# Experts as one hand-synchronised section with a branch over the third tile of tokens

## The chip, the cores and the metric

The program runs on one core of a Trainium2 chip. The metric is device time in microseconds, lower is better. Five engines take part, each with its own queue of instructions: TensorE (PE: matmul, PEld: loading of the stationary operand), VectorE (DVE), ScalarE (ACT), GpSimd (POOL) and SyncE (SP), which issues nearly all transfers from HBM. Matmuls write to eight PSUM banks; the granted clock of PE is 1.00 where it runs at 2.4 GHz.

## The reference

A two-layer transformer block stands in front (`first_block`), then a second one of two layers, whose last part is a mixture of experts. All of it is float32; only this last part is touched by the change:

```python
def moe_swiglu(h, router, w_gate, w_up, w_down):
    B, T, D = h.shape                                   # 1, 256, 1024
    ht = h.reshape(B * T, D)
    probs = jax.nn.softmax((ht @ router).astype(F32), axis=-1)      # 8 experts
    top_p, top_i = lax.top_k(probs, TOP_K)                          # TOP_K = 2
    top_p = top_p / jnp.sum(top_p, axis=-1, keepdims=True)
    gates = jnp.sum(jax.nn.one_hot(top_i, N_EXPERTS, dtype=F32) * top_p[..., None], axis=1).astype(h.dtype)
    out = jnp.zeros_like(ht)
    for e in range(N_EXPERTS):
        out = out + gates[:, e:e + 1] * swiglu(ht, w_gate[e], w_up[e], w_down[e])   # 1024 -> 1536 -> 1024
    return out.reshape(B, T, D)
```

Each of the 256 tokens goes to two of eight experts, so 512 places are shared out; how many an expert gets depends on the inputs.

## The kernel before

Everything up to the experts (attention, convolution, dense feed-forward) is left as it is. In `moe` the router counts the tokens of each expert; `places` writes one-hot matrices `oh` (which token stands in which place of an expert), and `gather` picks the tokens of three experts at a time by matmul into `xg`. An expert has room for `CAP` = 96 tokens, three tiles of 32 (`C32`, `NT`). If some expert got more than 96, the whole of `experts` is done again for the places behind (line 1736, a branch of all engines on `mosti`, the largest count).

`up(e)` walks over eight k-steps of two weight tiles (gate and up, 128 x 1536). A tile of tokens is only 32 wide, so the four column groups of PE each take a quarter of the weight's columns: per weight tile 3 tiles x 4 groups = 12 products, of 384 columns each (256 for expert 0, a third of whose columns are computed ahead of the router by `first_up`). `turn(e)` transposes the result, `down(e)` multiplies by twelve weight tiles of 128 x 1024: eight products each, four of 512 columns for the first two tiles of tokens and four of 256 columns for the third. `scatter(e)` brings the result back to token order by matmul, and VectorE adds it, times the gate, to `x`. All products of `up` and `down` go through `product`, so the profile shows them on line 1587. Every tile of tokens is computed, filled or not.

The order on PE is that of the code (`manual_schedule`): up(0), turn(0), then for each e: up(e) with scatter(e-2) between its steps, down(e-1) with turn(e) in it. Loads are issued by SP in an order that the framework's scheduler sets, as are the waits. Up weights have eight buffers (`mw`, 768 KB each, 512 KB for expert 0), down weights sixteen of 512 KB (`raw`, `wh`, `wl`, which the stages before used as well).

Of the kernel before, what the change touches and what calls it, by code (L numbers as in the profile page):

```python
# [6 lines left out]
F32 = mybir.dt.float32  # L7
# [34 lines left out]
MW_BUFS = 8  # L42
# [179 lines left out]


# [5 lines left out]
def build(tc, a, out, stages=None):  # L229
# [7 lines left out]
    with ExitStack() as es:  # L237
# [1215 lines left out]
        def moe(more, head, next_head):  # L1453
            hT = nrm["h"]
            with tc.tile_pool(name="moe", bufs=1) as sp:
# [12 lines left out]
                mosti = sp.tile([P, 1], I32, name="mosti")  # L1468
                trib = sp.tile([P, 2, P], BF16, name="trib")
# [5 lines left out]
                def router():  # L1475
# [36 lines left out]
                    V.tensor_copy(mosti, most)  # L1512
                    yield
# [39 lines left out]
                banks = {}  # L1553

                def bank(kind):

                    b, at = banks[kind]
                    banks[kind] = (b, (at + 1) % len(b))
                    return b[at]

                def experts(base, mid):

                    oh = sp.tile([P, 2, NE, P], F32R, tag="oh", name="oh")

                    def places(e):
                        for t in range(2):
                            V.tensor_scalar(oh[:, t, e], slots[:, base : base + P], pos[:, t, e : e + 1],
                                            sel[:, t, e : e + 1], op0=OP.is_equal, op1=OP.mult)

                    first = (0, 3, NE - 3)  # L1570
                    for e in range(3):
                        places(e)
                    made, turned, back = {}, {}, {}

                    def gather(e):

                        for k0 in range(0, KT, 2):
                            for k in (k0, k0 + 1):
                                p = bank("up")[:, : 3 * CAP]
                                for n, (t, part) in enumerate((t, part) for t in range(2) for part in (xh, xl)):  # L1580
                                    T.matmul(p, part[:, t, k * P : (k + 1) * P], oh[:, t, e : e + 3, :CAP], start=n == 0, stop=n == 3)  # L1581
                                o, g = xg[k // 4][:, k % 4], nrm["g"][:, k : k + 1]
                                A.activation(o, grp(p, 3), AF.Copy, scale=g) if k % 2 else V.tensor_scalar_mul(o, grp(p, 3), g)
                            yield

                    def product(o, l, w, first, last):
                        T.matmul(o, l, w, start=first, stop=last, skip_group_check=True)  # L1587

                    def up(e):


                        lo = 512 if e in mid else 0
                        n = (DE - lo) // 4
                        o = [[bank("up") for _ in range(2)] for _ in range(NT)]
                        for k in range(KT):
                            for m in range(2):
                                w = sp.tile([P, DE], F32, tag="mw", name="mw", bufs=MW_BUFS)
                                nc.sync.dma_start(w[:, : 4 * n], a["mo_u"][(e * KT + k) * 2 + m][:, lo:])
                                for t in range(NT):
                                    for g in range(4):  # L1600
                                        product(o[t][m][g * C32 : (g + 1) * C32, :n], xg[k // 4][:, k % 4, e - first[e // 3], t * C32 : (t + 1) * C32],
                                                w[:, g * n : (g + 1) * n], k == 0, k == KT - 1)
                            yield
                        made[e] = []
                        for t in range(NT):
                            u = sp.tile([P, 384], F32, tag="u", name="u", bufs=3)
                            A.activation(u[:, :n], o[t][0][:, :n], AF.Silu)  # L1607
                            V.tensor_mul(u[:, :n], u[:, :n], o[t][1][:, :n])
                            made[e].append(u)

                    def turn(e):

                        uT = sp.tile([P, DE // P, CAP], F32, tag="uT", name="uT", bufs=2)
                        turned[e] = uT
                        k1 = 0
                        if e in mid:
                            k1 = 4
                            u = mid[e]
                            for k0 in (0, 2):
                                p = bank("up")  # L1620
                                for k in (k0, k0 + 1):
                                    n = 0
                                    for t in range(2):
                                        for part in u:
                                            T.matmul(p[:, (k - k0) * S : (k - k0 + 1) * S], part[:, t, k * P : (k + 1) * P],
                                                     oh[:, t, :2], start=k == k0 and n == 0, stop=n == 3,
                                                     skip_group_check=True)
                                            n += 1
                                A.copy(uT[:, k0 : k0 + 2], grp(p, 2)[:, :, :CAP])
                        c = (DE // P - k1) // 4  # L1630
                        for t, u in enumerate(made.pop(e)):
                            p = bank("up")
                            for i in range(c):
                                T.transpose(p[:, i * P : (i + 1) * P], u[:, i * P : (i + 1) * P], ident)
                            A.copy(uT[:, k1:, t * C32 : (t + 1) * C32].rearrange("p (g c) n -> p c g n", c=c),
                                   p[:, : c * P].rearrange("p (c g n) -> p c g n", c=c, g=4))
                        p = bank("up")
                        for t in range(2):
                            T.transpose(p[:CAP, t * P : (t + 1) * P], oh[:, t, e, :CAP].bitcast(F32), ident)
                        ohT = sp.tile([P, 2, P], F32R, tag="ohT", name="ohT", bufs=2)  # L1640
                        A.copy(ohT[:CAP], p[:CAP, :S].rearrange("p (t n) -> p t n", t=2))
                        back[e] = ohT

                    def down(e):


                        uT = turned.pop(e)
                        acc = [bank("dn"), bank("dn")]
                        nk = DE // P
                        H = 2 * Q  # L1650
                        w = []
                        for kk in range(nk):
                            if kk % 4 == 0:
                                raw = wbuf("raw", 2 * D, F32, RAW_BUFS)
# [13 lines left out]
                            if kk % 2:  # L1668
                                yield
# [107 lines left out]
```

## Time and profile before

| | us |
|---|---|
| median of 3 runs | 1665.96 (1664.64 to 1666.89) |
| the profiled execution: time | 1666.39 |
| the profiled execution: span, first to last instruction | 1664.5 |
| first product of expert 0 | 1244.85 |
| last products of expert 7 end, copies begin | 1649.45 |

The mean granted clock is 0.984. A row of the chain reads: start, duration, engine, the tile's name, line, number of instructions; each f32 product counts twice on PE, with a weight load for each, as the hardware makes two passes of it. `pj` and `sm` are the two kinds of PSUM banks. A `q` behind an engine's name is its sequencer, which works ahead of the engine itself.

### The profile page before, as it was taken

How to read it: one execution, taken by the hardware profiler on the slowest of the kernel's cores; microseconds unless marked ns; L12 is line 12 of the kernel's file. 1: busy time of each engine (PE TensorE's matmuls, PEld its weight loads, DVE VectorE, ACT ScalarE, POOL GpSimd, SP SyncE). 2: the span in 40 equal slices, each digit the busy share in tenths (PEclk: the TensorE clock that was granted, in tenths of full speed). 3: DMA queues.
4: the chain of work that ended last, by engine and by line, in shares of the span. 5: the costliest groups of instructions: out<-in, count | busy, mean ns of one | idle time of the engine just before them, and what ended most of it. 6: DMA issues, size and time to landing. Idle time of an engine off the chain costs nothing.

```text
span 1664.5 us, 29813 instructions
## 1 busy us (share of the span) xinstructions
PE 1589.7 (96%) x12500; PEld 1245.9 (75%) x12500; DVE 888.3 (53%) x1547; ACT 734.7 (44%) x1318; POOL 121.6 (7%) x150
## 2 busy tenths in 40 slices
PE   7999999999999999987989999987999999999997
PEld 6878999878789999986879998977875444444443
DVE  6667877766558776876565555776460111111112
ACT  6646655555656555655464444555450110101001
POOL 2110000021000000151100000151100000000000
PEclk9999999999999999998999999998999999999998
DMA  7433655555426554432145554432369989998962
GB/s 284 152 120 126 214 178 192 171 179 183 145 78 215 192 179 161 163 136 74 45 176 190 197 178 165 154 132 60 149 237 409 395 329 370 373 372 339 374 232 78
DMA packets 68798, 336.86 MB, mean 202 GB/s; under 512 B 12816, under 2 KB 16112, under 8 KB 48048
## 3 DMA queue, kind: packets, MB, share of 16 engines
q1 hardware_dynamic: 57648, 327.70, 54.4%
q10 hardware_dynamic: 10272, 3.25, 0.8%
q0 software_dynamic: 736, 3.93, 0.6%
q8 instruction: 100, 1.64, 0.4%
q14 instruction: 42, 0.34, 0.1%
HBM read 332.03 MB, written 2.82 MB: 201 GB/s over the span
## 4 chain that ended last, share of the span: by engine, by line
PE 83%; issue 6%; DVE 4%; ACT 4%; POOL 2%; DMA 1%; ACTq 0%; POOLq 0%; DVEq 0%
PE pj L323 13%; PE pj L321 13%; PE pj L322 13%; PE sm L1587 12%; PE pj L1587 10%; PE sm L323 4%; PE sm L322 4%; PE sm L321 4%; PE sm L432 2%; DVE wl L314 1%; ACT wh L313 1%; PE sm L1220 1%; PE pj L1581 1%; PE sm L1229 1%; ACT hTh L333 1%
## 5 line engine op out<-in xcount | busy, mean ns | idle before, releaser
L314 DVE TENSOR_TENSOR wl<-raw,wh 128x1024 fp32r<-128x1024 f32 (+1 forms) x352 | 420.2, 1200 | 173.6 <-ACT wh L313 171.3
L313 ACT CAST wh<-raw 128x1024 fp32r<-128x1024 f32 (+1 forms) x352 | 359.5, 1028 | 216.2 <-PE pj L322 101.6
L321 PE MATMUL pj<-hTh,wh 128*128 128x256 f32 x1192 | 336.2, 282 | 0.0
L322 PE MATMUL pj<-hTl,wh 128*128 128x256 f32 x1192 | 335.8, 282 | 0.0
L323 PE MATMUL pj<-hTh,wl 128*128 128x256 f32 x1192 | 335.1, 282 | 0.0
L321 PEld LDWEIGHTS pj<-hTh,wh 128*128 128x128 f32 x1192 | 227.1, 191 | 1.1
L322 PEld LDWEIGHTS pj<-hTl,wh 128*128 128x128 f32 x1192 | 227.2, 191 | 0.9
L323 PEld LDWEIGHTS pj<-hTh,wl 128*128 128x128 f32 x1192 | 226.7, 191 | 0.2
L1587 PE MATMUL pj<-mw,xg 128*32 128x384 f32 (+1 forms) x2048 | 183.5, 473 | 0.0
L321 PE MATMUL pj<-wh,hTh 128*128 128x512 f32 (+1 forms) x368 | 141.9, 387 | 3.1 <-DVE mixl L335 1.5
L323 PE MATMUL pj<-wh,hTl 128*128 128x512 f32 (+1 forms) x368 | 139.0, 380 | 3.1 <-DVE hTl L335 3.0
L322 PE MATMUL pj<-wl,hTh 128*128 128x512 f32 (+1 forms) x368 | 139.5, 381 | 0.0
L1587 PEld LDWEIGHTS pj<-mw,xg 128*32 128x32 f32 x2048 | 65.3, 110 | 90.3 <-issue 83.3
L322 PE MATMUL sm<-wl,ph 128*128 128x512 f32 x264 | 103.2, 391 | 0.0
L321 PE MATMUL sm<-wh,ph 128*128 128x512 f32 x264 | 103.1, 391 | 0.0
L1587 PE MATMUL sm<-mw,xg 128*32 128x384 f32 (+1 forms) x1024 | 102.7, 473 | 0.0
L323 PE MATMUL sm<-wh,pl 128*128 128x512 f32 x264 | 102.0, 391 | 0.0
L843 DVE SCALAR_TENSOR_TENSOR u<-pj,tab_f,u 128x254 f32<-128x254 f32 (+1 forms) x176 | 82.7, 478 | 19.9 <-ACT u L841 18.2
L1607 ACT ACTIVATE u<-pj 128x384 f32<-128x384 f32 (+1 forms) x16 | 7.6, 477 | 180.4 <-PE pj L1587 180.4
L321 PEld LDWEIGHTS pj<-wh,hTh 128*128 128x128 f32 x368 | 70.7, 192 | 15.4 <-ACT hTh L333 2.5
L323 PEld LDWEIGHTS pj<-wh,hTl 128*128 128x128 f32 x368 | 70.3, 191 | 15.5 <-DVE hTl L335 6.0
L322 PEld LDWEIGHTS pj<-wl,hTh 128*128 128x128 f32 x368 | 70.6, 192 | 9.3
(435 smaller groups left out, 2266.9 us busy)
## 6 DMA issues: line engine op xcount, KB each, us to landing
mw<-in_mo_u SPq DMA_DIRECT2D x112, 768.0 KB, 7.0
raw<-in_up SPq DMA_DIRECT2D x44, 1024.0 KB, 4.9
raw<-in_mo_d SPq DMA_DIRECT2D x24, 1024.0 KB, 6.9
raw<-in_dn SPq DMA_DIRECT2D x22, 1024.0 KB, 4.8
raw<-in_fg_u SPq DMA_DIRECT2D x22, 1024.0 KB, 4.8
raw<-in_od_b SPq DMA_DIRECT2D x18, 1024.0 KB, 4.8
raw<-in_hy_b SPq DMA_DIRECT2D x16, 768.0 KB, 4.3
raw<-in_hy_a SPq DMA_DIRECT2D x12, 1024.0 KB, 4.8
```

Of the source, the lines that this page charges most:

```text
L313: A.copy(h, r)
L314: V.tensor_sub(m, r, h.bitcast(F32))
L321: T.matmul(o, lh, rh, start=first, stop=False)
L322: T.matmul(o, lh, rl, start=False, stop=False)
L323: T.matmul(o, ll, rh, start=False, stop=last)
L333: A.activation(oh, src, AF.Copy, scale=g)
L432: T.matmul(q, hT[j][:, k, ts_], w[f][k][v], start=t + k + i == 0, stop=k == KT - 1 and i == 2, skip_group_check=True)
L843: V.scalar_tensor_tensor(u[:, g, sh:], q[:, : S - sh], cw[:, f, g, wi : wi + 1], u[:, g, sh:], op0=OP.mult, op1=OP.add)
L1220: T.matmul(pq[:, i * P : (i + 1) * P], Am[:, i], U[:, i], start=i == 0, stop=True, skip_group_check=True)
L1229: T.matmul(pu[:, i * P : (i + 1) * P], Tt[:, i], Q[:, i], start=i == 0, stop=True, skip_group_check=True)
L1581: T.matmul(p, part[:, t, k * P : (k + 1) * P], oh[:, t, e : e + 3, :CAP], start=n == 0, stop=n == 3)
L1587: T.matmul(o, l, w, start=first, stop=last, skip_group_check=True)
```

## The change

The eight experts become one section of code in which the kernel sets all waits itself. A class `Hand` records every operation with its engine, what it reads and what it writes; from that it derives semaphore counts and emits the instructions engine by engine, with one semaphore per engine and one per load buffer. An operation is now a whole group of instructions (on PE all products of a k-step, or of two down tiles), and waits and signals once. The section stands in `tile_critical`: it begins when all engines have come to it. `places` and the first `gather` stay outside.

The router's counts go to `manyi`, and PE reads the eight into registers ahead of the section. In `up` for k > 0, and in `down` for all but the first two weight tiles, the products of the third tile of tokens stand behind a branch of PE alone: they are done if the expert has more than 64 tokens. With fewer, that tile's PSUM keeps what the first step wrote (the tokens there are zeros). They stand ahead of the other tiles' products of the step. The order among operations is kept; loads have an order of their own (`more`), nine up buffers instead of eight, and all down tiles are loaded one by one. The rare repetition for counts over 96 uses the same code without the hand-set waits and without branches.

```diff
-MW_BUFS = 8
+UP_SLOTS = 9
+DN_SLOTS = 16
+class Hand:
+    def emit(self, nc, engines, last):
...
+        for name, e in engines:
+            seen = {}
+            for eng, waits, go, lane, n in self.ops:
+                if eng == name:
+                    for w, v in waits.items():
+                        if v > seen.get(w, 0):
+                            e.wait_ge(sems[w], v)
+                            seen[w] = v
+                    go().then_inc(sems[lane], n)
+            if name == "SP":
+                for lane in last:
+                    e.wait_ge(sems[lane], self.count[lane])
...
+                    V.tensor_copy(manyi, p[:, 2 * NE : 3 * NE])
...
+                        self.order, self.busy = [("u", 0, j) for j in range(UP_SLOTS)], set()
+                    def more(self):
+                        d, u = [("d", 0, j) for j in range(nk)], [("u", 0, j) for j in range(UP_SLOTS, 2 * KT)]
+                        self.order, d = self.order + d[:4], d[4:]
+                        while u or d:
+                            self.order += u[:1] + d[:1]
+                            u, d = u[1:], d[1:]
+                        for e in range(1, NE):
+                            self.order += [("u", e, j) for j in range(2 * KT)]
+                            if e > 1:
+                                self.order += [("d", e - 1, j) for j in range(nk)]
+                        self.order += [("d", NE - 1, j) for j in range(nk)]
+                        self.feed()
...
+                    def third(self, e, go):
+                        if self.many is None:
+                            return go()
+                        with T.If(self.many[e] > 2 * C32):
+                            go()
...
+                            def go(k=k, tiles=tiles):
+                                if k == 0:
+                                    return tiles(range(NT))
+                                self.third(e, lambda: tiles((2,)))
+                                return tiles((0, 1))
+                            self.op("PE", go, [*w, ("xg", k)], [b for bs in o for b in bs])
+                            self.used(w)
...
+                            def go(k0=k0, halves=halves, quarters=quarters):
+                                self.third(e, quarters) if k0 else quarters()
+                                return halves()
...
-                        for g in range(4):
-                            o, p = y[2 * C32 : CAP, g * Q : (g + 1) * Q], acc[1][g * C32 : (g + 1) * C32, :Q]
-                            V.tensor_copy(o, p) if g % 2 else A.copy(o, p)
+                                (("ACT", "DVE")[g % 2], y[2 * C32 : CAP, g * Q : (g + 1) * Q], banks[b1][g * C32 : (g + 1) * C32, :Q], b1)
+                                for g in range(4)]:
...
+                main = Experts(0, mid, at_once)
+                with tc.manual_schedule(engines=MAN):
+                    main.places()
+                    main.feed()
+                    rest(main.gather(0))
+                main.many = [nc.values_load(manyi[:1, e : e + 1], engines=[mybir.EngineType.PE], min_val=0, max_val=S) for e in range(NE)]
+                hand = Hand()
+                main.op = hand.op
+                main.more()
+                main.run()
+                with tc.tile_critical():
+                    hand.emit(nc, (("SP", nc.sync), ("ACT", A), ("DVE", V), ("PE", T)), [("out", t, n) for t in range(2) for n in range(2)])
```

On PE, the end of up(1) and the beginning of down(0) read so before; L1587 is `product`, `mw` the up weights, `raw` and `wh` the down weights, and the shape 32x384 is that of one product:

```order
L1587 MATMUL pj<-mw,xg 32x384 x8
L1587 MATMUL sm<-mw,xg 32x384 x4
L1587 MATMUL pj<-mw,xg 32x384 x4
L1587 MATMUL sm<-raw,uT 32x512 x4
L1587 MATMUL sm<-raw,uT 32x256 x4
```

The same place now; L1712 are the up products, L1802 and L1795 the down products of the third tile and of the other two, L1671 the branch:

```order
L1671 COMPARE_AND_BRANCH
L1712 MATMUL pj<-up_12149,xg 32x384 x4
L1712 MATMUL pj<-up_12150,xg 32x384 x4
L1671 UNCONDITIONAL_BRANCH
L1712 MATMUL pj<-up_12149,xg 32x384 x4
L1712 MATMUL sm<-up_12149,xg 32x384 x4
L1712 MATMUL pj<-up_12150,xg 32x384 x4
L1712 MATMUL sm<-up_12150,xg 32x384 x4
L1802 MATMUL sm<-wh,uT_12141 32x256 x4
L1802 MATMUL sm<-wl,uT_12141 32x256 x4
```

The third tile's products of both weight tiles of a step have moved to its front, between a condition and a jump.

On SP, the loads of expert 0 and those behind them read so before (line 1598 loads up weights, lines 1655 and 1659 down weights; the first eight up tiles and sixteen down tiles stand ahead of this):

```order
L1659 DMA wl<-in_mo_d 128x1024
L1659 DMA wh<-in_mo_d 128x1024
L1598 DMA mw<-in_mo_u 128x1024 x8
L1598 DMA mw<-in_mo_u 128x1536 x24
L1655 DMA raw<-in_mo_d 128x2x1024
```

Now, with the section's beginning (line 1942 is the jump into it, for which SP waits for all engines; all loads are on line 1662):

```order
L1894 NO_OP
L1942 UNCONDITIONAL_BRANCH
L1662 DMA wh<-in_mo_d 128x1024
L1662 DMA wl<-in_mo_d 128x1024
L1662 DMA wh<-in_mo_d 128x1024
L1662 DMA wl<-in_mo_d 128x1024
L1662 DMA up_12146<-in_mo_u 128x1024
L1662 DMA wh<-in_mo_d 128x1024
L1662 DMA up_12147<-in_mo_u 128x1024
L1662 DMA wl<-in_mo_d 128x1024
```

The down tiles, which were sent before the experts began, have moved behind the section's beginning, among the remaining seven up tiles of expert 0.

On PE, between the last products of the gather and the first of expert 0, there is now this (line 1889 reads a count into a register; five more such reads stand among the gather's products):

```order
L1689 MATMUL pj<-oh,xl 128x288
L1889 TENSOR_LOAD manyi
L1889 ISA x2
L1889 TENSOR_LOAD manyi
L1889 ISA x2
L1889 TENSOR_LOAD manyi
L1889 ISA x2
L1942 UNCONDITIONAL_BRANCH
L1712 MATMUL pj<-up_12146,xg 32x256 x4
```

The row of products is cut there by three reads and by the jump at which all engines meet.

## Rows read from the trace of the kernel before

**Rows 1.** The page: busy time by engine, and the queue of instruction packets.
```profile
PE 1589.7 (96%) x12500; PEld 1245.9 (75%) x12500; DVE 888.3 (53%) x1547; ACT 734.7 (44%) x1318; POOL 121.6 (7%) x150
...
q8 instruction: 100, 1.64, 0.4%
```

**Rows 2.** Stretches: busy us of PE, PEld, DVE, ACT, POOL; clock, DMA share, GB/s.
```profile
1240.00:1280.00 40.00, 40.00 (x587) 24.36 (x589) 5.12 (x12) 6.67 (x15) 0.00 (x0) 1.00 1.01 401
...
1360.00:1400.00 40.00, 40.00 (x455) 17.84 (x451) 6.62 (x10) 4.73 (x10) 0.00 (x0) 1.00 0.87 314
```

**Rows 3.** PE's waits from 1236 us on: total us, times, longest.
```profile
PE pj L1688 <- ACT yh L327: 3.4, 1, 3.4
```

**Rows 4.** The chain in order of time: start us, us, what; experts 0 and 1.
```profile
1244.85 0.57 PE pj L1587 x8
...
1245.85 0.86 PE pj L1587 x16
1246.71 0.43 PE sm L1587 x8
...
1270.11 1.29 PE pj L1587 x16
1271.40 0.65 PE sm L1587 x8
...
1299.78 10.32 PE sm L1587 x128
```

**Rows 5.** Sequencers at lines 1735, 1736, 1773: ns min/median/max, first and last start us.
```profile
L1735 PEldq EVENT_SEMAPHORE  x6: 51/51/51, 1654.5 to 1655.0; - x6
L1735 PEldq TENSOR_LOAD <-mosti x1: 492/492/492, 1655.1 to 1655.1; - x1
L1735 SPq FUSED_REGOPS  x1: 186/186/186, 1239.4 to 1239.4; - x1
...
L1736 POOLq COMPARE_BRANCH  x1: 45/45/45, 1237.2 to 1237.2; - x1
L1773 POOLq DRAIN  x3: 40/107/723, 1237.4 to 1664.3; - x3
...
L1736 PEldq COMPARE_BRANCH  x1: 3775/3775/3775, 1655.7 to 1655.7; - x1
L1736 ACTq COMPARE_BRANCH  x1: 54/54/54, 1660.3 to 1660.3; - x1
L1736 ACTq EVENT_SEMAPHORE  x1: 17/17/17, 1663.6 to 1663.6; - x1
```

**Rows 6.** SP's issues in order of time, 1190 to 1260 us: start, us, what.
```profile
1190.28 3.88 SPq L1598 DMA_DIRECT2D mw<-in_mo_u  x8
...
1213.44 11.36 SPq L1655 DMA_DIRECT2D raw<-in_mo_d  x2
...
1241.31 0.40 SPq L1659 DMA_DIRECT2D wh<-in_mo_d  x1
```

**Rows 7.** Two stretches with loads queued, columns as in rows 2.
```profile
1203.00:1206.00 3.00, 0.88 (x4) 0.38 (x3) 1.50 (x4) 1.55 (x5) 0.57 (x1) 1.00 1.03 426
...
1245.00:1248.00 3.00, 3.00 (x60) 1.82 (x56) 0.00 (x0) 1.67 (x2) 0.00 (x0) 1.00 1.03 421
```

**Rows 8.** The up weights' loads, from issue to landing.
```profile
DMA to landing us min/median/max: 3.6/6.9/11.5
```

**Rows 9.** The end in order of time: start, us, engine, line, what, idle before.
```profile
1649.45 0.58 ACT L1673 COPY y<-sm 64x512 f32<-64x512 f32 x1 [15.86 <-PE sm L1587]
...
1652.09 1.04 ACT L327 CAST yh<-y 96x1024 fp32r<-96x1024 f32 x1 [0.50 <-DVE y L1677]
...
1656.91 2.07 ACTq L1693 DMA_DIRECT2D out_x<-x  x2
...
1657.17 0.63 PE L1689 MATMUL sm<-yl,ohT 96*128 96x512 f32 x1
```

**Rows 10.** Transfers by line: issues, KB each, median us to landing.
```profile
out_x<-x ACTq DMA_DIRECT2D x2, 256.0 KB, 3.1
```

More of the change, by code (lines that the diff above doesn't have):

```diff
@@ L1551, in first_up @@
                     mid[0] = (uh, ul)
[L1553 to L1575, printed above, removed]
+                first = (0, 3, NE - 3)
@@ L1611, in turn @@
[L1611 to L1642, printed above, removed]
@@ L1692, in scatter @@
                                 if e == NE - 1:
-                                    (nc.sync, nc.scalar)[t].dma_start(out[t][:, c], x[:, t, c])
+                                    self.op(("SP", "ACT")[t], lambda c=c, t=t: (nc.sync, nc.scalar)[t].dma_start(out[t][:, c], x[:, t, c]),
+                                            [("x", t, n)], [("out", t, n)], load=("out", t, n))
                                 yield
-                    rest(gather(0))
-                    for e in range(3, NE):
-                        places(e)
@@ L1713, in experts, with run @@
-                    last = down(NE - 1)
-                    next(last)
-                    rest(scatter(NE - 2, "up"))
-                    rest(last)
-                    rest(scatter(NE - 1, "up"))
+                    def run(self):
+                        for e in range(NE):
+                            side = self.scatter(e - 2) if e >= 2 else iter(())
+                            for k, _ in enumerate(self.up(e)):
+                                if k % 2 == 1:
+                                    next(side, 0)
+                                    next(side, 0)
+                            more_ = self.gather(first[(e + 1) // 3]) if e % 3 == 2 else iter(())
+                            if e:
+                                for k, _ in enumerate(self.down(e - 1)):
+                                    next(more_, 0)
+                                    if k == 3:
+                                        self.turn(e)
+                            else:
+                                self.turn(e)
+                        last = self.down(NE - 1)
+                        next(last)
+                        rest(self.scatter(NE - 2, "up"))
+                        rest(last)
+                        rest(self.scatter(NE - 1, "up"))
@@ L1719, in moe, with at_once @@
+                def at_once(eng, go, reads=(), writes=(), load=None):
+                    go()
                 mid = {}
+                ups = [sp.tile([P, DE], F32, name=f"up{i}") for i in range(UP_SLOTS)]
                 with tc.manual_schedule(engines=MAN):
-                    first, route = first_up(mid), router()
-                    next(first)
+                    first_, route = first_up(mid), router()
+                    next(first_)
                     next(route)
-                    next(first)
+                    next(first_)
@@ L1725, in moe @@
                     next(route)
-                    next(first)
+                    next(first_)
                     next(route)
                     shares()
-                    rest(first)
-                banks["up"] = ([ps("pj") for _ in range(4)] + [ps() for _ in range(2)], 0)
-                banks["dn"] = ([ps() for _ in range(2)], 0)
+                    rest(first_)
+                us = [sp.tile([P, 512], F32, tag="u", name="u", bufs=3) for _ in range(3)]
+                yh, yl = (t.rearrange("p t c -> p (t c)") for t in mid[0])
```

263 lines of the change are left out of this document (184 added, 79 removed).

## The prediction

> **What bounds the kernel now.** I read the page's busy shares first: TensorE (PE) is busy 96% of the span [rows 1]. An average says little, so next the stretches of the last part, the eight experts: from 1240 us on PE is busy 40.00 of every 40 us at full clock, while the transfers swing between 401 and 314 GB/s [rows 2]. A busy PE could still hide waits, since ends of matmuls are modelled; the list of PE's waits settles it. In this part no PE wait for a transfer is listed, and the longest wait of all is 3.4 us, for ScalarE at the very end [rows 3]. So from the first product of expert 0 at 1244.85 us [rows 4] to the end of the last one's products at 1649.45 us [rows 9] the experts are a string of PE work, 404.6 us or 50.6 us an expert, and whatever leaves PE there leaves the span, until the loads become late.
>
> **What is removed.** An expert's tokens lie in three tiles of 32. In the up products one weight tile takes 1.29 + 0.65 = 1.94 us for three tiles of tokens [rows 4], 0.645 us each. A k-step has two weight tiles, so a skipped third tile saves 1.29 us; k = 0 is always done, seven steps remain: 9.0 us. Expert 0 has narrower weights (256 columns, 0.86 + 0.43 us): 0.43 x 2 x 7 = 6.0 us. In the down products 128 PE instructions, eight weight tiles, take 10.32 us [rows 4], 1.29 us each; the third tile is 256 of the 768 columns, 0.43 us, and ten of twelve are conditional: 4.3 us. How many experts skip, no profile tells; the reference does: with its own draw of inputs the router sends 61, 74, 68, 70, 62, 49, 70 and 58 tokens to experts 0 to 7. Four (0, 4, 5, 7) have at most 64. Sum: 6.0 + 3 x 9.0 + 4 x 4.3 = **50.3 us** of PE work, on the path.
>
> **What it costs, part by part.**
> *Entering the section.* PE's sequencer now reads eight counts into registers within the gather. One read takes 0.49 us, and the register work behind it 0.19 us on SyncE [rows 5]: 8 x 0.68 = 5.4 us. Products already queued cover some of it (four reads stand in the middle of the gather, three behind it). Then all engines meet, and behind that meeting are queued expert 0's products on PE and every further load on SP. The ninth early load stands ahead of router-stage weights. Bounds: 2 us (three reads alone) and 8 us (all, and a hand-over); I take **5**, nearer to the full count of reads, since the meeting has no cover.
>
> *The loads behind the meeting.* Before, SP had issued eight weight tiles of expert 0 and, from 1213 to 1241 us, all 16 down tiles for which there is room (three double loads and ten single ones; [rows 6] has the first and the last). Now it has nine tiles out and stops until the meeting. It then sends four down tiles, and the seven missing up tiles with a down tile between each two, so the last tile of expert 0 is the 17th load. What rate? With loads queued unpaced, 426 and 421 GB/s [rows 7], against 401 in the long stretch in which PE paced them [rows 2]; I take 412. 17 x 0.524 MB / 412 GB/s = 21.6 us; the quickest landing took 3.6 us [rows 8], 1.7 more than 0.786 MB take at that rate. Up products of expert 0 end 21.6 + 1.7 + 1.7 = 25 us after the meeting, where the shortened work alone needs 2.6 + 7 x 1.72 = 14.6: about 10.5 us of waiting. The first pair of expert 1 is loads 20 and 21: 24.2 + 3.8 + 1.7 = 29.7 us, against PE ready at 28.4. Together **12** (10 at 425 GB/s, 14 at 390). Expert 0 thus gains nothing in its up products.
>
> *Later loads.* An expert's weights are 18.87 MB, 45.8 us. A full expert takes PE 50.6 us, a skipping one 37.3. Experts 4 and 5 fall 17 us behind the loads, 7 another 8.5; full slots (9 up, 16 down tiles, 15.5 MB) are a lead of some 37 us at best. Over all, 146.8 MB less the nine early tiles, 142.1 MB, remain at the meeting, 345 us: from about 1250 to 1595 us, against PE's end near 1622; but during experts 1, 2, 3 and 6 the loads stand still some 5 us each for want of slots. That leaves 7 us of slack, so local waits only: **4** (0 to 15).
>
> *Branches.* Twelve conditions an expert, 96 in all, and 48 jumps behind the bodies that are done. The nearest row is GpSimd's short jump: 45 ns, the next instruction 0.2 us after it began [rows 5]. On PE it lies under queued products: its sequencer was through with all issues by 1654.5 us, when its last products began only at 1657.17 [rows 5, 9], 2.6 us ahead, as long as the products between two conditions. Where PE had waited for a load there is no cover. Bounds 0 and 96 x 0.2 = 19; I take **3**.
>
> *Leaving the section.* Registers are now read after the output transfers have landed: ScalarE's last one is issued at the end of a stretch that lasts from 1656.91 to 1658.98 us [rows 9] and takes 3.1 to land [rows 10]; a read of some 0.5 behind that lets ScalarE's long jump begin near 1662.6 us instead of 1660.3 [rows 5], 2.3 later. Against that the copies of y no longer alternate between two engines (2.6 us from the first to the next step [rows 9], some 1.3 of it gone). **1** (-1 to 5).
>
> Sum on the profiled execution: 1664.5 - 50.3 + 5 + 12 + 4 + 3 + 1 = 1639.2, plus 1.9 us outside the span: **1641 us**. That execution is 0.4 us above the median, which I leave.
>
> **The rivals.**
> *A. Each condition stalls the instruction fetch; slower.* Long jumps do: PE's at the end took 3.78 us, and ScalarE's next instruction came 3.2 us after its own [rows 5]. If every one of the 96 cost some 3.5 us less 2.6 us of cover, that is 86 us, and the time 1641 - 7 + 86 = 1720 us. It decides from an exposed 0.3 us a condition (28 us of net gain over 96). Against it: GpSimd's short jump, and a skip spans only 32 PE instructions (eight products of two loads and two matmuls each), an eighth of the 250 that one instruction packet holds (100 packets, 25,000 PE instructions [rows 1]). Chance 0.08; another 0.05 that only jumps over a packet's edge or waits without cover cost, 10 to 25 us more.
> The Trainium skill speaks against the change here (Runtime: NRT & Kernel Launch, Instruction fetch mechanics): a taken branch whose target lies outside the two fetched pages waits for a fetch, which is why kernels are better unrolled. By that rule the end jump stalls, as in the row, and a jump of 32 instructions mostly doesn't; no run here shows one on PE.
>
> *B. The loads bind throughout.* If the 6 KB rows do no better than about 370 GB/s, 142.1 MB take 384 us: landing at 1634, then 4 us to the last product, 16 of tail, 2 outside: 1656 us. The windows at 421 and above speak against it, though they held loads of 4 KB rows. Chance 0.10.
> At 358 GB/s it would be 397 us and 1669 us, no change; that end has 0.02 of the 0.10.
> The Trainium skill's HBM Reference (Specifications) names just these 358 GB/s as effective per core. It also gives about 425 for a core that streams alone, and the trace agrees with that (426).
>
> *C. No tile is empty in the inputs run.* Then only costs stand: 5 for the meeting, 5 for expert 0's loads, 3 and 1: 1680 us. Chance 0.03; four counts have a margin of two tokens or more.
>
> **How the numbers follow.** Forecast as summed: 0.74. Its own bounds: every cost at its low end (2 + 10 + 0 + 0 - 1) gives 1627; later waits at 15 with branches at half their bound give 1659. The range, 1627 to 1660, holds the forecast and most of B. A measurement of this kernel can tell some 0.2%, 3.3 us. Faster: 0.74, most of B (0.08) and part of the jumps at edges (0.02), 0.84. Within: 0.05. Slower: A and C, 0.11.
>
> **What would show it.** In the changed trace PE should issue 12 groups fewer for experts 0, 4, 5, 7 alone. Expert 0's up products should stretch to about 25 us with waits for loads. The period of experts 4 and 5 should fall to 37 to 46 us, that of 2, 3 stay near 51. Transfers should be near 400 GB/s in the last third. Gaps between a condition and the next product on PE should be under 0.3 us where no load is late. If all experts' periods grow by tens of us, A is right; if PE waits for loads in every expert, B. A meeting that costs over 10 us, or granted clock lost while PE waits for loads, would make the sum wrong without either.

## The result, and the profile after

The changed kernel takes 1643.22 us (median of 4 runs, 1642.03 to 1645.21); the kernel before, run beside it, 1665.56. The ratio is 0.9866, 95% interval 0.9849 to 0.9884. The forecast was 1641 us in a range of 1627 to 1660. The profiled execution of the changed kernel took 1642.03 us, its span 1640.2.

First the page of the changed kernel, busy time by engine and the queue of instruction packets, which answer to [rows 1]:

```profile
PE 1544.0 (94%) x11732; PEld 1224.4 (75%) x11732; DVE 887.2 (54%) x1548; ACT 733.7 (45%) x1318; POOL 121.7 (7%) x150
...
q8 instruction: 100, 1.64, 0.4%
```

TensorE (PE) has 768 matmuls fewer, 192 for each of four experts: 7 steps x 2 weight tiles x 4 products and 10 down tiles x 4 products are 96, and each product is two PE instructions. So the skip does what it says, for four experts. The instruction packets are as many as before.

The stretches of the last part, columns as in [rows 2]:

```profile
1240.00:1280.00 40.00, 26.51 (x341) 16.14 (x343) 3.94 (x9) 6.46 (x15) 0.00 (x0) 0.91 0.85 338
1360.00:1400.00 40.00, 40.00 (x444) 18.32 (x447) 7.21 (x12) 5.74 (x12) 0.00 (x0) 1.00 0.80 312
1440.00:1480.00 40.00, 40.00 (x471) 16.76 (x467) 7.07 (x11) 5.11 (x11) 0.00 (x0) 1.00 1.02 413
1480.00:1520.00 40.00, 36.17 (x367) 15.37 (x359) 6.50 (x12) 6.61 (x15) 0.00 (x0) 1.00 1.02 413
```

Where [rows 2] had PE busy 40.00 of 40 us, it is now idle for 13.5 us in the first of these stretches, and for 3.8 us in expert 5 (the last one, in which the transfers run at 413 GB/s without a pause, a DMA share of 1.02). PE's waits from 1236 us on, which answer to [rows 3]; there no wait for a transfer was listed:

```profile
PE pj L1712 <- DMA up<-in_mo_u: 17.4, 11, 3.3
PE pj L1828 <- DVE ul L1817: 4.2, 1, 4.2
PE sm L1802 <- DVE y L1815: 1.8, 1, 1.8
PE pj L1712 <- SPq L1894: 1.3, 1, 1.3
```

Expert 0's up products in order of time (start us, us, engine, line, what; the idle time before in brackets), from the first one after the meeting to the first product of expert 1:

```profile
1243.52 0.29 PE L1689 MATMUL pj<-oh,xl 128*128 128x288 f32 x1
1245.15 0.64 PE L1712 MATMUL pj<-up,xg 128*32 128x256 f32 x8 [1.34 <-SPq L1894]
...
1255.80 0.64 PE L1712 MATMUL pj<-up,xg 128*32 128x256 f32 x8 [2.67 <-DMA up<-in_mo_u]
...
1261.04 1.08 PE L1712 MATMUL pj<-up,xg 128*32 128x256 f32 x8 [3.31 <-DMA up<-in_mo_u]
...
1266.32 0.64 PE L1712 MATMUL pj<-up,xg 128*32 128x256 f32 x8 [1.90 <-DMA up<-in_mo_u]
...
1271.30 1.08 PE L1712 MATMUL pj<-up,xg 128*32 128x256 f32 x8 [3.04 <-DMA up<-in_mo_u]
...
1278.91 0.85 PE L1712 MATMUL pj<-up,xg 128*32 128x384 f32 x8 [0.71 <-ACT ohT L1781]
```

The meeting itself costs 1.34 us. Then come four waits for up tiles, 10.92 us together, and behind two of them the same eight products take 1.08 us instead of 0.64. The clock column of narrow stretches, shown for the first of the two, says why (columns as in [rows 2]):

```profile
1258.00:1260.00 2.00, 0.00 (x0) 0.00 (x0) 0.00 (x0) 0.00 (x0) 0.00 (x0) 1.00 1.02 412
1260.00:1262.00 2.00, 0.96 (x12) 0.50 (x16) 0.00 (x0) 0.00 (x0) 0.00 (x0) 0.65 1.02 410
1262.00:1264.00 2.00, 2.00 (x24) 0.86 (x20) 0.00 (x0) 0.00 (x0) 0.00 (x0) 0.50 1.03 410
```

PE did nothing from 1258 to 1260 us; when it started again the granted clock was 0.65 and then 0.50, the lower of the two levels, 1.2 GHz.

The conditions (line 1671) and the reads of the counts (line 1889) on PE's sequencer, columns as in [rows 5]:

```profile
L1671 PEldq COMPARE_BRANCH  x96: 65/138/436, 1246.5 to 1620.5; - x96
```
```profile
L1889 PEldq TENSOR_LOAD <-manyi x8: 294/301/489, 1236.0 to 1242.6; - x8
L1889 PEldq FUSED_REGOPS  x8: 146/146/160, 1236.6 to 1243.0; - x8
```

### The profile page after: what moved, and what is told of

It is laid out like the page before. It is cut to its first block, busy times and chain, and to the rows that moved or that the text cites. A ratio compares the mean times of both kernels' runs of the same rounds, so it can differ in the third digit from the quotient of the medians.

```text
span 1640.2 us, 28381 instructions
## 1 busy us (share of the span) xinstructions
PE 1544.0 (94%) x11732; PEld 1224.4 (75%) x11732; DVE 887.2 (54%) x1548; ACT 733.7 (45%) x1318; POOL 121.7 (7%) x150
## 4 chain that ended last, share of the span: by engine, by line
PE 79%; issue 6%; ACT 4%; DVE 4%; DMA 3%; POOL 2%; SPq 1%; ACTq 0%; POOLq 0%; DVEq 0%
PE pj L372 13%; PE pj L370 13%; PE pj L371 13%; PE pj L1712 7%; PE sm L1795 5%; PE sm L372 4%; PE sm L371 4%; PE sm L370 4%; PE sm L1712 4%; DMA up<-in_mo_u 2%; PE sm L481 2%; PE sm L1802 2%; DVE wl L363 1%; ACT wh L362 1%; PE sm L1269 1%
## 5 line engine op out<-in xcount | busy, mean ns | idle before, releaser
L1712 PE MATMUL pj<-up,xg 128*32 128x384 f32 (+1 forms) x1712 | 156.5, 483 | 19.7 <-DMA up<-in_mo_u 17.4
L1712 PEld LDWEIGHTS pj<-up,xg 128*32 128x32 f32 x1712 | 55.7, 111 | 101.9 <-issue 100.1
L1712 PE MATMUL sm<-up,xg 128*32 128x384 f32 (+1 forms) x912 | 90.0, 478 | 0.0
L1732 DVE TENSOR_TENSOR u<-u,pj 128x384 f32<-128x384 f32 (+1 forms) x16 | 8.2, 533 | 139.7 <-ACT u L1731 139.7
```

Of the source, the lines that this page charges most:

```text
L1712: i = T.matmul(banks[o[t][m]][g * C32 : (g + 1) * C32, :n], xg[k // 4][:, k % 4, e - first[e // 3], t * C32 : (t + 1) * C32], ups[w[m][1]] ...
L1732: self.op("DVE", lambda u=u, p=lin: V.tensor_mul(u, u, p), [o[t][1], ("us", i)], [("us", i)])
```

## The experiments

Two measures are used. One is the median. The other is the time from expert 0's first up product to the end of the span in the profiled run, called **the last part** below: it leaves out what moves before (that first product came between 1243.05 and 1247.38 us in these runs). Before it is 1664.5 - 1244.85 = 419.65 us, in the changed kernel 1640.2 - 1245.15 = 395.05 us. It comes from one execution and is rough by 1 to 2 us: behind the last wait for `ul` alone these runs take between 11.7 and 13.6 us. The ratio is to the kernel before on the same chip.

| run | median us | ratio, 95% | last part us |
|---|---|---|---|
| again: the changed kernel | 1643.40 | 0.9876, 0.9859 to 0.9892 | 395.10 |
| static: skip without conditions | 1643.92 | 0.9869, 0.9853 to 0.9886 | 395.87 |
| always: section, no skip | 1678.09 | 1.0079, 1.0062 to 1.0095 | 432.58 |
| true: section, conditions that hold | 1678.07 | 1.0083, 1.0066 to 1.0100 | 432.15 |
| order: missing up tiles first | 1641.89 | 0.9858, 0.9841 to 0.9874 | 395.05 |
| early: 8 down tiles ahead | 1634.40 | 0.9809, 0.9791 to 0.9827 | 387.92 |
| full0: expert 0 never skips | 1648.25 | 0.9893, 0.9876 to 0.9909 | 402.74 |
| banks: early, other banks | 1632.61 | 0.9806, 0.9790 to 0.9822 | 385.01 |
| narrow: fewer bytes behind expert 0 | 1635.00 | 0.9822, 0.9807 to 0.9837 | 387.41 |
| lead: another order throughout | 1644.08 | 0.9879, 0.9863 to 0.9894 | 396.56 |
| all: 10 early, order, banks | 1634.55 | 0.9818, 0.9805 to 0.9832 | 384.99 |
| all12: 12 early | 1634.44 | 0.9811, 0.9796 to 0.9826 | 387.27 |

**What do the conditions cost?** Three runs on one chip, with the changed kernel once more as their yardstick.

> The changed kernel once more, as the yardstick of this group. Both theories: 1643 us, within 2 us.

```diff
-                        with T.If(self.many[e] > 2 * C32):
-                            go()
+                        if e not in (0, 4, 5, 7):
+                            go()
```


> The changed kernel without conditions on TensorE: the products of the third tile are left out of experts 0, 4, 5 and 7 when the program is built, and stand in the others; the registers are still read. Theory 'the conditions are hidden' (in the trace of the changed kernel TensorE's products of expert 4 leave no room for them, and the 96 compare-and-branch of 65 to 436 ns lie beside queued products): the time of the changed kernel, 1643 us within 2. Rival as predicted, 3 us exposed: 1640 us. Rival instruction fetch, at least 0.1 us each for 96: under 1633 us.

```diff
-                        with T.If(self.many[e] > 2 * C32):
-                            go()
+                        go()
```


> The section with waits of its own, but no conditions: the third tile is always done, the registers are still read. It prices the section alone. Theory 'the start lacks loads' (17 loads of expert 0 behind the meeting): before plus about 1 for the meeting, 8 to 9 of waiting in expert 0's up products (they end some 25 us after the meeting either way, against 20.6 of work), 1 at the end, nothing later since a full expert takes 50.6 us and its loads 45.8: 1676 us (1673 to 1680). Rival 'the wait at the start is made by the skipping itself' (expert 0 outruns its loads only because it skips): within 2 us of before, 1665 to 1668.

```diff
-                        with T.If(self.many[e] > 2 * C32):
+                        with T.If(self.many[e] > 0):
```


> As the section alone, but with the 96 conditions, made so that each holds (a count over 0): every body is done, and the jump behind each body with it. Against the section without conditions it is the price of 96 compares and 96 jumps over nothing. Theory 'hidden under the queue': the same time within 2 us, some 1676 us. Rival 'an instruction that is not skipped pays as well', the 0.14 us of the median compare-and-branch exposed 96 times: 13 us more. Rival fetch at the jump, 0.3 us or more each: 29 us more or worse.

The same skip without any condition takes 1643.92 us against 1643.40; 96 conditions that hold take 1678.07 against 1678.09 without. By the medians, 96 conditions cost nothing that shows, whether they jump or not. One thing blurs this a little: the two runs without conditions spend 2.4 to 3.6 us outside the span, where the changed kernel and the run in which all hold spend 1.8 to 1.9; why stays open. By the spans alone the conditions cost 0.7 us in either pair (medians 1641.55 against 1640.9, and 1676.25 against 1675.5), less than the 2.4 to 4.2 us by which executions of one kernel differ. In the run where all hold they are shorter, by the same view as above:

```profile
L1671 PEldq COMPARE_BRANCH  x96: 65/65/87, 1244.4 to 1654.0; - x96
```

With the 48 that jump the longest is 436 ns, and none of it shows on PE: from expert 0's first product to its first down product, which stands behind expert 1's up products, it is 64.72 us with conditions and 64.73 without; expert 4's up products, up to the next down products, take 24.47 and 24.46. The run without skip prices the section: 432.58 - 419.65 = 12.9 us of the last part, 13.7 us by the medians (1678.09 against 1664.35). Expert 0, from its first up product to that of expert 1, is 10.5 us of it (34.34 us against 23.83), though nothing is skipped. Expert 1's first product in the chain of the kernel before, then expert 0's and expert 1's in this run:

```profile
1268.68 0.78 PE pj L1587 x8
```
```profile
1245.32 0.64 PE L1711 MATMUL pj<-up,xg 128*32 128x256 f32 x8 [1.38 <-SPq L1893]
1279.66 0.85 PE L1711 MATMUL pj<-up,xg 128*32 128x384 f32 x8 [0.71 <-ACT ohT L1780]
```

The waits of the run:

```profile
PE pj L1711 <- DMA up<-in_mo_u: 5.3, 3, 2.3
PE pj L1827 <- DVE ul L1816: 4.2, 1, 4.2
PE sm L1801 <- DVE y L1814: 1.8, 1, 1.8
```

Three waits for up tiles sum to 5.3 us, and the clock falls behind two of them here too: the step behind each takes 4.41 us instead of 2.58. Most of the other 2.4 us lies at the end, 17.0 us from the last products to the end of the span against 15.05. The rival, that only the skipping makes PE outrun its loads at the start, is out. The whole skip is worth 432.58 - 395.05 = 37.5 us, where the sum had 50.3 us of products.

**What holds the start: the order of the loads, or their bytes?**

```diff
-                        self.order, d = self.order + d[:4], d[4:]
+                        self.order += d[:2] + u
+                        d, u = d[2:], [("u", 1, j) for j in range(2 * KT)]
                         while u or d:
                             self.order += u[:1] + d[:1]
                             u, d = u[1:], d[1:]
-                        for e in range(1, NE):
+                        for e in range(2, NE):
...
```


> The changed kernel with one thing different: behind the meeting SyncE sends two down tiles and then the seven missing up tiles of expert 0 in one go; the other ten down tiles of expert 0 follow, one behind each up tile of expert 1. Theory 'the order of the loads makes the start late' (the last up tile is the 9th load instead of the 17th): expert 1 starts some 12 us earlier than at 1279, near 1266; some of it is given back in expert 1's up products, whose last tile is the 35th load (35 x 1.27 us behind 1246.5, 1291); 6 to 7 us remain, 1637 us (1634 to 1641). Rival 'what counts is the sum of the loads, since they bind later anyway': 1643 us, expert 4 and 5 wait longer. In both the granted clock should stay at 1.00 through expert 0, if it fell for the waits.

```diff
+EARLY = 8
...
-                        self.order, self.busy = [("u", 0, j) for j in range(UP_SLOTS)], set()
+                        self.order, self.busy = [("u", 0, j) for j in range(UP_SLOTS)] + [("d", 0, j) for j in range(EARLY)], set()
...
-                        d, u = [("d", 0, j) for j in range(nk)], [("u", 0, j) for j in range(UP_SLOTS, 2 * KT)]
+                        d, u = [("d", 0, j) for j in range(EARLY, nk)], [("u", 0, j) for j in range(UP_SLOTS, 2 * KT)]
```


> As the run with the other order, and eight down tiles of expert 0 are sent ahead of the section, into the 30 us from 1214 to 1245 in which the queues of the changed kernel are empty (they go into the buffers that come free first). Theory 'it is loads that the start lacks': no wait for more than 1 us in expert 0 and 1, expert 1 starts near 1264 instead of 1279, granted clock 1.00, 1628 us (1625 to 1632). Rival 'the meeting waits for what is under way': first up product later than 1247 and little gain, 1640 us. Rival 'the later loads take it back' (from 1440 on transfers run at 412 GB/s without a pause): 1635 us or more, with more than 6.5 us of waiting in experts 4 to 7.

```diff
+                        if e == 0:
+                            return go()
                         with T.If(self.many[e] > 2 * C32):
```


> The changed kernel, but expert 0 always does its third tile, without a condition: up 6.0 us and down 4.3 us of products more. Theory 'expert 0's up products go by the loads': expert 1 starts under 1 us later than in the changed kernel (1279.7 against 1278.9), the down products cost their 4.3: 1648 us, or down to 1645 if the waits of experts 4 and 5 give way. Rival 'the skipping in expert 0 is worth what its products take': 1653 us.

With the other order expert 1 starts 22.7 us behind expert 0's first product instead of 33.8, as expected, and the granted clock stays at 1.00. But all of it is given back in expert 1's up products. PE's products there, in order of time:

```profile
1283.27 0.84 PE L1712 MATMUL sm<-up,xg 128*32 128x384 f32 x8
1287.04 2.14 PE L1712 MATMUL pj<-up,xg 128*32 128x384 f32 x24 [2.93 <-DMA up<-in_mo_u]
...
1293.37 0.85 PE L1712 MATMUL pj<-up,xg 128*32 128x384 f32 x8 [2.26 <-DMA up<-in_mo_u]
```

Five such waits sum to 9.3 us, and the last part is 395.05 us, that of the changed kernel. My expectation of 6 to 7 us had counted expert 1's up tiles at 0.524 MB; they are 0.786. Then 19 tiles of 0.524 and 16 of 0.786 MB, 22.5 MB, must land behind the meeting before expert 1's up products can end, in this order as in the changed kernel's, and that is 55 us at 412 GB/s. From expert 0's first product to the end of expert 1's up products it is 64.1 us in this run and 64.7 in the changed kernel. The rival holds: bytes, not order. Whether the lower clock cost time in the changed kernel this run doesn't show, since its loads stand otherwise. There expert 1 follows without a wait for loads, and expert 0's last step takes 3.37 us instead of 1.72, so up to 1.65 us of the clock's fall can lie on the path.

Fewer bytes behind the meeting do help. The changed kernel transfers next to nothing from 1214 us to the meeting; eight down tiles sent there use that time (this run has the other order as well, and takes the down buffers in the order in which they come free). That stretch in the changed kernel, then in the run with eight early tiles (columns as in [rows 2]):

```profile
1214.00:1245.00 31.00, 28.19 (x154) 22.45 (x152) 20.80 (x61) 12.88 (x26) 0.56 (x1) 1.00 0.00 1
```
```profile
1214.00:1245.00 31.00, 29.39 (x158) 23.58 (x157) 22.45 (x62) 14.07 (x28) 0.56 (x1) 1.00 0.38 137
```

8 x 0.524 MB are 10.2 us at 412 GB/s; against the run with the other order alone the median falls by 7.5 us, the last part by 7.1. Expert 1 now starts 23.05 us behind expert 0's first product, and expert 1's up products end 55.2 us behind it, 8.9 us earlier than in that run. I had expected 1628 us, and no wait over 1 us in experts 0 and 1; one of 1.70 us remained in expert 0. Waits for loads in the later experts, 6.6 us in 5 and 7, keep the time at 1634.4, close to the rival by which the later loads take it back. In expert 5 the clock fell again, behind a wait of 2.30 us.

Where expert 0 never skips the median is 1648.25 us, 4.85 more than with its skip, as expected (4.3 for its down products, and from expert 0's first product to expert 1's 34.39 us instead of 33.76). Its up products' skip, 6.0 us of work, is worth 0.6. The last part of this run is 7.7 us longer; what exceeds the 4.9 stands elsewhere, 1.2 us in expert 4's up products, which wait 0.95 us for a load there, and 1.3 behind the last wait for `ul`.

**What keeps the skip of the later experts from its full worth?**

```diff
+                            if (e, j) >= ((1, UP_SLOTS) if kind == "u" else (1, 4)):
+                                dst, src = dst[:, : D // 2], src[:, : D // 2]
```


> The changed kernel, but of each weight tile behind expert 0's (from the second use of a buffer on) only the first 512 columns are transferred, a third of an up tile and half of a down tile; the products run over the whole buffers, old values included. Theory 'what the skipping does not give back behind expert 0 is waiting for loads': the 6.5 us of waits in experts 4, 5 and 7 go, the start stays as it is, 1637 us. Rival 'skipped products are worth less than they take' (something other than loads holds TensorE): 1643 us.

```diff
+                        u = [("u", e, j) for e in range(1, NE) for j in range(2 * KT)]
+                        self.order, u = self.order + u[:UP_SLOTS], u[UP_SLOTS:]
                         for e in range(1, NE):
-                            self.order += [("u", e, j) for j in range(2 * KT)]
-                            if e > 1:
-                                self.order += [("d", e - 1, j) for j in range(nk)]
-                        self.order += [("d", NE - 1, j) for j in range(nk)]
+                            self.order, u = self.order + u[: 2 * KT], u[2 * KT :]
+                            self.order += [("d", e, j) for j in range(nk)]
```


> The changed kernel with another order of loads from expert 1 on: nine up tiles of the next expert, then the twelve down tiles, then the other seven up tiles, so that SyncE does not stand at an up tile whose buffer is in use while down buffers come free. Theory 'the queue stands still at 1320 to 1400 us for the order, not for lack of buffers': over 380 GB/s there, the 6.5 us of waits in experts 4, 5 and 7 go, 1637 us. Rival 'the buffers are full, and the order changes nothing': 1643 us.

With fewer bytes behind expert 0 the last part is 7.6 us shorter, the median 8.4, and no wait for a load is left behind expert 0; the four that this view still has are expert 0's:

```profile
PE pj L1714 <- DMA up<-in_mo_u: 11.0, 4, 3.5
```

The up products of experts 5 and 7, up to the next down products, now take 24.47 us each, as expert 4's do here and in the changed kernel, where they take 29.21 and 28.20. So what was lost there is loads, in experts 5 and 7; expert 4 loses nothing. The other order, in contrast, does fill the queue and gains nothing. Two stretches of the changed kernel, then of that run (columns as in [rows 2]):

```profile
1320.00:1340.00 20.00, 20.00 (x227) 7.95 (x220) 4.17 (x6) 2.35 (x4) 0.00 (x0) 1.00 0.56 206
1380.00:1400.00 20.00, 20.00 (x232) 8.21 (x228) 4.21 (x6) 1.04 (x1) 0.00 (x0) 1.00 0.76 278
```
```profile
1320.00:1340.00 20.00, 20.00 (x228) 7.59 (x220) 4.17 (x6) 2.90 (x6) 0.00 (x0) 1.00 1.03 411
1380.00:1400.00 20.00, 20.00 (x232) 8.20 (x228) 4.89 (x7) 1.66 (x3) 0.00 (x0) 1.00 0.78 294
```

The half of the theory on the queue is right in the first stretch, 411 GB/s instead of 206; in the second it is 294 instead of the 380 expected. The half on the waits is wrong: the time is 1644.08 us. Expert 5's last up products in that run, in order of time, and SP's loads of its last seven up tiles with eight of expert 6's, say why:

```profile
1485.43 0.85 PE L1712 MATMUL pj<-up,xg 128*32 128x384 f32 x8 [0.31 <-issue]
...
1489.31 0.85 PE L1712 MATMUL pj<-up,xg 128*32 128x384 f32 x8 [1.09 <-DMA up<-in_mo_u]
...
1492.95 0.85 PE L1712 MATMUL pj<-up,xg 128*32 128x384 f32 x8 [0.85 <-DMA up<-in_mo_u]
...
1497.14 0.85 PE L1712 MATMUL pj<-up,xg 128*32 128x384 f32 x8 [1.41 <-DMA up<-in_mo_u]
```
```profile
1475.05 25.27 SPq L1662 DMA_DIRECT2D up<-in_mo_u  x15
```

A skipping step takes PE 2.58 us, and its two up tiles, 1.57 MB, take 3.82 us at 412 GB/s; the steps here follow each other by 3.6 to 4.2 us. There are only nine up buffers, so the last seven tiles of an expert can be sent only as its own steps free them: the first goes out at 1475.05 us, just behind expert 5's first step, which ends at 1474.8. From then on they come at the pace of transfers. Seven at that pace would be there near 1490 us by an estimate (7 x 1.91, and 1.7 for the landing), but the last pair's products begin at 1497.14; how much of that is down tiles sent before them and expert 6's tiles beside them was not separated. A lead in down buffers doesn't help, nor is it the sum of all bytes that binds: in this run the transfers thin out earlier (309 GB/s from 1580 to 1600 us against 409), while the waits for loads in experts 5 and 7 stay (7.6 us against 6.5). That the number of up buffers is the cause is thus argued, not shown: more of them were not tried, for want of room beside the sixteen down buffers.

**Is there more at the end or at the start?**

```diff
-                        b0, b1 = self.bank("dn"), self.bank("dn")
+                        b0, b1 = (self.bank("up" if e == NE - 1 else "dn") for _ in range(2))
```


> As the run with eight early tiles, and the last expert's down products go to two of the six other PSUM banks, so that they need not wait for the copies of y of the expert before. Theory 'the 1.8 us wait of TensorE for y ahead of the last down products is on the path': 1.8 us less than that run, 1626 us. Rival 'something else is late there' (the turned u of expert 7, or the loads): no difference within 1 us.

The next has both orders of loads, these banks, and two early tiles more:

```diff
-EARLY = 8
+EARLY = 10
```


> The three together: ten down tiles of expert 0 ahead of the section, the order of loads of the run before, the last expert's down products in other banks. If the gains add up: 1632.6 of the run with eight early tiles and other banks, less 6.6 of later waits, less some 2 at the start by two more early tiles: 1624 us (1621 to 1628). If the later waits stay: 1631 us.

```diff
-EARLY = 10
+EARLY = 12
```


> As that, with all twelve down tiles of expert 0 ahead of the section; the last two are issued near 1238 to 1241 us, when their buffers come free. Theory 'the meeting waits for what is under way': the first up product comes 1 to 3 us later, and the time is that of ten tiles or 2 us more, 1624 to 1626. Rival 'loads are all that counts at the start': 1 to 2 us less than with ten, 1622.

In other banks the 1.8 us wait for y is gone, and a new one of 1.6 us for `ul` takes its place ahead of the product that puts expert 6's tokens back:

```profile
PE sm L1829 <- DVE ul L1818: 4.2, 1, 4.2
PE pj L1829 <- DVE ul L1818: 1.6, 1, 1.6
```

So 0.2 us is all that this view gives it. The medians differ by 1.8 us, but the runs of the one reach from 1632.04 to 1637.10 and of the other from 1631.23 to 1634.28: not told apart. The run with all three together misses its 1624 us: 1634.55, a last part of 384.99 like that of the one before, since the order brought nothing, and the waits of experts 5 and 7 stay (8.0 of 11.0 us listed). All twelve tiles early are the same within the spread; whether the meeting came later for them stays open, since the first up product's time moves as much from run to run. Of these four none is told from another; the lowest median, 1632.61 us, is 0.66% under the changed kernel's 1643.40 and beats both kernels. More than eight early tiles thus gave nothing that shows.

## Why the prediction was right

The sum came within 2.2 us of the median. Its largest term was right, its mechanism too. That it came so close is luck in part: two of the smaller terms were 3 to 4 us too high (entering, branches) and two 3 to 4 us too low (both terms on loads), and they cancelled.

*Removed, 50.3 us: right in what it counts.* Expert 4, which doesn't wait, shows it, from its first up product to expert 5's, with expert 3's full down products between; before, then in the changed kernel:

```profile
1422.83 0.83 PE L1587 MATMUL sm<-mw,xg 128*32 128x384 f32 x8
...
1473.30 0.83 PE L1587 MATMUL pj<-mw,xg 128*32 128x384 f32 x8
```
```profile
1428.78 0.83 PE L1712 MATMUL sm<-up,xg 128*32 128x384 f32 x8
...
1470.21 0.83 PE L1712 MATMUL pj<-up,xg 128*32 128x384 f32 x8
```

This fell from 50.47 to 41.43 us, 9.04 us for the 9.0 counted. Four experts skip, by 192 matmuls each.

*Entering, 5 us: too high.* From the gather's first product to expert 0's it is 4.39 us before (the timeline has expert 0's first product at 1244.78, the chain at 1244.85) and 5.77 now:

```profile
1240.39 0.30 PE L1581 MATMUL pj<-oh,xh 128*128 128x288 f32 x1
```
```profile
1239.38 0.30 PE L1689 MATMUL pj<-oh,xh 128*128 128x288 f32 x1
```

The 1.4 us more are the meeting, 1.34 us in PE's wait for SP. The sum had taken 0.68 us for each read from one row; they take 0.30 and 0.15 us each, and the gather's matmuls run on beside them (the prediction counted four reads there and three behind; it is five and three).

*Loads behind the meeting, 12 us: right in kind, too low.* From expert 0's first product to expert 1's it is 33.76 us; the shortened work is 23.83 - 6.0 = 17.8, so 15.9 us are added. Expert 0's up products were to end 25 us behind the meeting; they ended 29.5 us behind the first of them (1274.67). The last pair came after 26.1 us where the sum had 23.3 for the 17th load, and the products behind it ran at the lower clock, 1.65 us longer, which was not in the sum; the prediction had named such a loss as a sign of being wrong, but had put nothing on it. With the meeting these two terms are 17 predicted and 15.9 + 1.4 = 17.3 found.

*Later loads, 4 us of 0 to 15: mis-sized.* The listed waits of experts 5 and 7 are some 6.5 us, and taking the bytes away gives 7.6 to 8.4. From its first up product to expert 6's, expert 5 takes 47.2 us where the forecast had at most 46 (that stretch holds work that expert 4's does not; it was 55.8 before). The sum weighed all bytes against a lead in full buffers. What it lacked, as far as the runs show, is the pace inside one skipping expert, whose last seven up tiles can't be sent ahead and take 1.91 us each or more.

*Branches, 3 us: nothing that shows.* Rival A is out: 96 conditions change 1643.40 to 1643.92 when taken away, and 1678.09 to 1678.07 when added. The Trainium skill (Runtime: NRT & Kernel Launch, Instruction fetch mechanics) has a taken branch wait for a fetch where its target lies outside the two fetched pages; the trace agrees with that, with a jump of 32 PE instructions (436 ns at most, hidden) and the long one at the end (3.80 us; 3.78 in [rows 5]).

*Leaving, 1 us: right.* From the last expert's products to the span's end it is 1640.2 - 1624.34 = 15.9 us against 1664.5 - 1649.45 = 15.05.

*Rival B* was half the truth: transfers do bind, but in experts 0, 5 and 7 alone, and at 413 GB/s. The Trainium skill's HBM Reference (Specifications) has about 358 GB/s as one core's share with both cores of a pair streaming, and about 425 for a core that streams alone; this program ran on one core, and from 1440 to 1520 us it held 413 with 6 KB and 4 KB rows, so the trace agrees with the second figure, and rival B's far end, which went by the first, did not come. *Rival C* is out for these inputs; but the run that never skips is what it would be, 1678 us, and the forecast for it was 1680.

The balance of the last part closes. The section costs 12.9 us. Of the skip's 50.3, expert 0's up products lose 6.0 - 0.6 = 5.4 and the later experts 7.6 to their loads, so 37.3 should be left, and 37.5 is. 12.9 - 37.5 = -24.6 is the difference from 419.65 to 395.05. That it closes to 0.2 us is luck, since each last part is rough by 1 to 2 us.

## What to carry to other kernels

Skipping work on the bounding engine pays only down to the pace of the loads, and that pace counts within the section too: compare one step's work with the transfer time of the tiles of that one step, and ask how many buffers of that very kind cover the difference (that more of them help is argued here, not shown). A section with waits of its own must not begin with an empty queue: count the bytes that must land before its second stage ends, and send as many as buffers allow ahead of the meeting (eight tiles were worth 7.5 us here, ten and twelve no more). In the two runs that changed only the order, the same bytes in another order moved a wait, not the end.

## What the runs showed of the hardware

- A compare-and-branch on PE takes 65 ns where it falls through (65/65/87 over 96) and up to 436 ns where some jump over 32 instructions, and none of it shows in PE's time, even in expert 0 where PE waited for loads (64.72 us with conditions, 64.73 without).
- Granted clock behind a wait: it fell to 0.50 behind waits of 3.31 and 3.04 us in expert 0, and of 2.31 and 2.32 us in the run that never skips, but stayed at 1.00 through 2.67 us in expert 0 of the changed kernel itself and through 2.93 us in expert 1 of the run with the other order. So in these runs the length of the wait alone doesn't tell whether the clock falls; what does stays open.
- In the changed kernel every 20 us from 1440 to 1600 us moved 409 to 416 GB/s, on one core, with PE at work beside it.
